# Twelve adaLN column steps moved from the projection blocks into the samples' unit of the recurrence

## The chip, the cores and the metric

The kernel runs on one core of one Trainium2 chip. The metric is the device time of one execution in microseconds (us). TensorE is called PE here (PEld is its weight load), VectorE DVE, ScalarE ACT, GpSimd POOL, and SyncE SP. SP issues nearly all DMA transfers of this kernel, one after the other in program order.

## The reference, cut to what matters

One layer of a streaming encoder: 2048 prompt positions and 8 samples of 16 positions. A small matrix product (adaLN) turns the 9 condition vectors (1 prompt, 8 samples) into six vectors of 1024: shift, scale and gate of the mixer (`sh1, sc1, g1`) and of the FFN (`sh2, sc2, g2`). The second half of them is needed late: `g1` at the output projection, `sh2` and `sc2` at the second norm, `g2` at the end.

```python
mod = jax.nn.silu(c) @ p['w_ada'][l] + p['b_ada'][l]
sh1, sc1, g1, sh2, sc2, g2 = jnp.split(mod[:, None], 6, axis=-1)
h = _rmsnorm(x, p['norm_mix'][l]) * (1.0 + sc1) + sh1
proj = h @ p['w_in'][l]
u_gate, u_lru, p_rwkv, u_s5 = jnp.split(proj, IN_SPLITS, axis=-1)
...
y_b, rw_shift, rw_s = _rwkv7(p_rwkv, rw_shift, rw_s, ...)      # the recurrence
...
mix = jnp.concatenate([y_a, y_b, y_c], axis=-1) @ p['w_out'][l]
x = x + g1 * mix
h2 = _rmsnorm(x, p['norm_ffn'][l]) * (1.0 + sc2) + sh2
f, ffn_buf = _conv_ffn(h2, ffn_buf, ...)
x = x + g2 * f
```

## The kernel before, in words

The work runs in four parts.

**Setup** computes `sh1` and `sc1` (tiles `sh1`, `gs1`), the vectors that the first norm needs.

**Projection blocks.** Four blocks of 512 positions (the first also holds the samples). Each block has 20 column groups of `w_in`: `gemm_cols` issues 24 matmuls into the tile `pgm` (a product in three parts, L558 to L560), then calls `bg_step`, which takes one or two closures from the list `bg` and runs them. That list holds work that needs no fixed place: tables for the S5 group, the sample states, the first chunks of the recurrence, and 32 adaLN steps (`ada_step`). One adaLN step makes 128 columns: it loads 512 KB of `w_ada` (tile `aw`, one buffer, L1218; the step asks for the next load when it is done), multiplies (8 matmul instructions into `pada`, L159, two records each in the profile), copies to `part` on ACT, multiplies again with a selector (`padm`, L164 or L172), and DVE adds the bias (L167 or L177). The projections of the RWKV group go on to `prep` (four calls a block, one after the other, `qr` and `bk` with one buffer each), whose last matmul writes `pb` (L693).

**Recurrence.** Nine units: unit 0 is the samples, then eight halves of the prompt's blocks. A unit has four chunks `c`. Ahead of a unit stands `inverse` (a triangular inverse in many small DVE instructions, L1190 to L1205, fed by a DMA round trip `tscr`, `tb`), and `join`, which turns its result into `xt`. In a unit PE does, per chunk: `st_q` (L1477 in unit 0), `st_u` (`um`, L1495), a part of the masks of a later unit (`pam`, L1155, operands `qr`, `bk` loaded by SP), `st_m` (`mm`), `st_y` (`ry`, L1529), and the next chunk's `pre_pe` (`pvt`, `pbk`) and `pre_v` (`ry`, L1457). Between these stands `fill`, three times a chunk, which steps the inverse of the next unit and pieces of the output projection.

In unit 0 PE's order is exactly the order of the code (`manual_schedule`). Everywhere else, and on the other engines in unit 0 too, a scheduler fixes each engine's order when the kernel is built. Each engine then works through its list in that order and waits at an instruction whose inputs or buffers aren't ready. `ppt` in the recurrence gives tiles from a pool of two PSUM buffers, in turn.

**FFN.** From about 1640 us on, with its own norm, up and down projections.

Of the kernel before, what the change touches and what calls it, by code (L numbers as in the profile page):

```python
# [9 lines left out]
F32 = mybir.dt.float32  # L10
# [9 lines left out]
P = 128  # L20
D = 1024
KD = D // P
# [14 lines left out]
def hymba_step(ctx: ExitStack, tc: tile.TileContext, I: dict, O: list):  # L37
    nc = tc.nc
    V, S, G, PE, SY = nc.vector, nc.scalar, nc.gpsimd, nc.tensor, nc.sync
# [3 lines left out]
    NBLK = SEQ // 512  # L43
# [4 lines left out]
    def act(out, in_, func=AF.Copy, **kw):  # L48
        S.activation(out, in_, func, **kw)  # L49
# [102 lines left out]
    s5fin = ct([P, 2, 8, 8], "s5fin")  # L152
    dcol = ct([P, 16], "dcol")

    def ada_cols(q, c_0, n, wt, psum, part, small):

        pg_ = psum("pada")
        for k in range(KD):
            PE.matmul(pg_[32 * (k % 4):32 * (k % 4) + 32, :n], lhsT=cT[:, k, :], rhs=wt[:, k, :],  # L159
                      start=(k < 4), stop=(k >= 4), skip_group_check=True)  # L160
        act(part[:, :n], pg_[:, :n])
        pm = psum("padm")
        if q in (2, 5):
            PE.matmul(pm[0:9, :n], lhsT=sel, rhs=part[:, :n], start=True, stop=True)  # L164
            bg_, gr_ = small("abg", n), small("agr", n)
            SY.dma_start(out=bg_, in_=I["b_ada"][:, q * D + c_0:q * D + c_0 + n].to_broadcast([9, n]))
            V.tensor_tensor(gr_, pm[0:9, :n], bg_, ADD)  # L167
            SY.dma_start(out=gmd[:, q // 3, c_0:c_0 + n], in_=gr_)
            return
        nm = n // P  # L170
        for m in range(nm):
            PE.matmul(pm[:, m * 9:m * 9 + 9], lhsT=part[:, m * P:(m + 1) * P], rhs=sel, start=True, stop=True)  # L172
        pv_ = pm[:, :nm * 9].rearrange("p (m j) -> p m j", j=9)
        c8 = c_0 // P
        b0 = offs["b_ada"] + q * 8 + c8
        dst = {0: sh1, 1: gs1, 3: sh2, 4: gs2}[q][:, c8:c8 + nm, :]
        V.tensor_tensor(dst, pv_, vec[:, b0:b0 + nm].unsqueeze(2).to_broadcast([P, nm, 9]), ADD)  # L177
        if q in (1, 4):
            n0 = offs["norm_mix" if q == 1 else "norm_ffn"] + c8
            V.scalar_tensor_tensor(dst, dst, 1.0, vec[:, n0:n0 + nm].unsqueeze(2).to_broadcast([P, nm, 9]), ADD, MUL)  # L180
# [269 lines left out]
    with ExitStack() as cm:  # L450
# [7 lines left out]
        def ppt(name):  # L458
            return pp.tile([P, 512], F32, tag="pp", name=name)
# [15 lines left out]
        bg = []  # L475
# [733 lines left out]
            sto["xs"] = xs_  # L1209


        adaq = [(q, c * P) for q in (2, 4, 3, 5) for c in range(KD)]
        adaw = []

        def ada_load(i):
            q, c_0 = adaq[i]
# [4 lines left out]
        def ada_step(i):  # L1221
            q, c_0 = adaq[i]
            if i == 0:
                ada_load(0)
            wt = adaw[i]
            part = lp.tile([P, P], F32, tag="apart", name="apart")
            ada_cols(q, c_0, P, wt, ppt, part, lambda t_, n: lp.tile([9, n], F32, tag=t_, name=t_))
            if i + 1 < len(adaq):
                ada_load(i + 1)

        w_load()
# [12 lines left out]
        bg += [late_work] + [lambda l=l: tab_phasor(l) for l in ((0, 1, 2, 3, 4), (5,), (6,), (7,))]  # L1244
        bg += [lambda k=k: tab_wk(k) for k in range(8)] + [tab_load]
        bg += [lambda k=k: tab_toep(k) for k in range(0, 8, 2)]
        bg += [lambda i=i: ada_step(i) for i in range(len(adaq))]
        for blk in range(NBLK):
            units = ["s", "p"] if blk == 0 else ["p"]
            s5_in(blk)  # L1250
            if blk == min(2, NBLK - 1):
                bg = s0_steps + bg + row_steps
            if blk % 2 == 1:
                bg = s5_half(blk // 2) + bg
            if blk + 1 < NBLK:
                load_x(blk + 1)
            lo12 = shift_mix(blk, 12)
            lo13 = shift_mix(blk, 13)
            xwa = {}
            for u in units:  # L1260
                T = NS if u == "s" else 512
                c0_ = 0 if u == "s" else NS + blk * 512
                lo_ = lo12[u]
                act(lo_[0:64, :T], lo_[0:64, :T], AF.Tanh)

                su = "s" if u == "s" else ""
                xw = xmp.tile([P, T], F32R, tag="xw" + su, name="xw", bufs=1)
                xa = xmp.tile([P, T], F32R, tag="xa" + su, name="xa", bufs=1)
                act(xw[0:64, :], lo_[0:64, :T])
                act(xa[64:128, :], lo_[64:128, :T])  # L1270
                V.tensor_tensor(xw[64:128, :], lo_[0:64, :T], xw[0:64, :].bitcast(F32), SUB)
                V.tensor_tensor(xa[0:64, :], lo_[64:128, :T], xa[64:128, :].bitcast(F32), SUB)
                xwa[u] = (xw, xa)
                sg = lo13[u]
                act(sg[:, :T], sg[:, :T], AF.Tanh, scale=0.5)
                V.tensor_scalar(sg[:, :T], sg[:, :T], 0.5, 0.5, MUL, ADD)
                SY.dma_start(out=sgd[:, c0_:c0_ + T], in_=sg[:, :T])
            if blk == NBLK - 1:
                lru(blk, 0)
                lru(blk, 1)  # L1280
            for hp in range(4):
                xr, xk, xv = shift_mix(blk, hp), shift_mix(blk, 4 + hp), shift_mix(blk, 8 + hp)
                for u in units:
                    ui = 0 if u == "s" else blk + 1
                    prep(hp, u, ui, xr[u], xk[u], xv[u], *xwa[u])
            for j in range(2):
                if blk + 1 < NBLK:
                    lru(blk, j)
                    if j == 0:
                        norm_full(blk + 1)  # L1290
            if blk + 1 < NBLK:
                norm_split(blk + 1)
            if blk + 1 == NBLK - 1:
                xin.close()
                cxq = ctx.enter_context(ExitStack())
                xqs.append(cxq.enter_context(tc.tile_pool(reuse_waits="tile", name="xq", bufs=3, side="right")))
                rap.append(cra.enter_context(tc.tile_pool(reuse_waits="tile", name="ra", bufs=1, side="right")))
                msks.append(rat([P, 2, P], "mask_s"))
                G.tensor_copy(msks[0], mask)
                for row in range(2):  # L1300
                    for e in range(2):
                        G.memset(msks[0][64 * row:64 * row + 32, e, :].rearrange("p (s t) -> p s t", t=32)[:, 1:4:2, :], 0.0)
                st0 = a_start()
                inv0 = inverse(0, st0)
                bg += [lambda c=c: a_chunk(0, st0, c) for c in range(4)] + [lambda: next(inv0, None)] * 10
            if blk == NBLK - 1:
                bg_step(len(bg))
# [3 lines left out]
    if True:  # L1311
        ow = crs.enter_context(tc.tile_pool(reuse_waits="tile", name="ow", bufs=1))
        po = crs.enter_context(tc.tile_pool(reuse_waits="tile", name="po", bufs=1, space=PSUM))
# [10 lines left out]
        def ot(shape, name, bufs=1):  # L1324
            return ow.tile(shape, F32, tag=name, name=name, bufs=bufs)
# [461 lines left out]
        wos = [(0, p_, load_wo, i) for i, p_ in enumerate((0, 1, 2, 3, 5, 7, 10, 11))]  # L1787
        wos += [(p_ // 12, p_ % 12, split_wo, i) for i, p_ in enumerate((4, 7, 10, 12, 13, 14, 15, 16))]
        gnq = []
        jn = None  # L1790
        FL, FC = 3, 6
        for n, un in enumerate(units):
            with (tc.manual_schedule(engines={mybir.EngineType.PE}) if n in (0,) else ExitStack()):
                nx = units[n + 1] if n + 1 < len(units) else None
                nx2 = units[n + 2] if n + 2 < len(units) else None
                for c in range(4):
# [4 lines left out]
                    def fill(pos):  # L1801

                        nonlocal inv, jn
                        for u_, p_, fn, k in wos:
                            if (u_, p_) == (n, pos):
                                fn(k)
                        if n == 3:
                            step(srg)
                        if inv is not None:
                            if not step(inv[1]):  # L1810
                                jn = join(inv[0], sto[inv[0]])
                                inv = None
                        if jn is not None and pos >= JP and not step(jn):
                            jn = None
                        if gnq and n > 0 and not step(gnq[0]):
                            gnq.pop(0)
                        o_step(OS)
                        if n == len(units) - 1:
                            if pos == FL:
                                nst.pop(0)()  # L1820
                            if pos >= FC:
                                for fn in nst[:5]:
                                    fn()
                                del nst[:5]
# [43 lines left out]
    with ExitStack() as cf:  # L1868
# [467 lines left out]
        with tc.manual_schedule(engines={ENG.PE, ENG.DVE, ENG.Activation, ENG.Pool, ENG.SP}):  # L2336
# [172 lines left out]
            turn, out = state_items(hal2.rearrange("p t m -> p (t m)"), 88, p_fc.rearrange("l b t (k p) -> (l b t k) p", p=P))  # L2509
# [9 lines left out]
            for k, (which, q, first, final) in enumerate(prods):  # L2519
# [56 lines left out]
                if xt is not None:  # L2576
                    t, n = done_of(k)
# [41 lines left out]
```

## Time and profile before

| | |
|---|---|
| median of 3 runs | 3210.2 us (3208.82 to 3218.33) |
| the profiled execution | 3212.56 us, its span 3210.8 us |
| PE busy | 2876.3 us, 90% of the span |
| DVE busy | 2115.3 us, 66% |
| ACT busy | 1373.9 us, 43% |
| POOL busy | 594.1 us, 19% |
| mean granted clock of PE | 0.917 |

The span runs from the first to the last instruction of the profiled execution. Busy times are sums over instructions; PE's are modelled, so a busy PE can still be a slow one. The granted clock is a share of 2.4 GHz: 1.00 is that level, 0.50 is 1.2 GHz.

### The profile page before, as it was taken

How to read it: one execution, taken by the hardware profiler on the slowest of the kernel's cores; microseconds unless marked ns; L12 is line 12 of the kernel's file. 1: busy time of each engine (PE TensorE's matmuls, PEld its weight loads, DVE VectorE, ACT ScalarE, POOL GpSimd, SP SyncE). 2: the span in 40 equal slices, each digit the busy share in tenths (PEclk: the TensorE clock that was granted, in tenths of full speed). 3: DMA queues.
4: the chain of work that ended last, by engine and by line, in shares of the span. 5: the costliest groups of instructions: out<-in, count | busy, mean ns of one | idle time of the engine just before them, and what ended most of it. 6: DMA issues, size and time to landing. Idle time of an engine off the chain costs nothing. (4 is left out here: it accounts for less than half of the span.)

```text
span 3210.8 us, 44566 instructions
## 1 busy us (share of the span) xinstructions
PE 2876.3 (90%) x16111; PEld 2292.9 (71%) x16111; DVE 2115.3 (66%) x3944; ACT 1373.9 (43%) x2436; POOL 594.1 (19%) x787
## 2 busy tenths in 40 slices
PE   5887996989977899999975999999599999899998
PEld 3766663756656778778754888888488887678876
DVE  6765774556666636766426777788888888364676
ACT  2445545553633324333444454444444444233222
POOL 1211201111234556666530000000000000000001
PEclk9988997989955779998977999999799999999999
DMA  6666554755574344443453333324333333576564
GB/s 182 140 104 151 162 150 139 216 145 172 160 197 135 82 127 135 133 123 100 121 174 112 114 107 117 101 79 120 107 107 99 104 103 118 185 241 224 175 218 172
DMA packets 595200, 453.45 MB, mean 141 GB/s; under 512 B 128032, under 2 KB 513700, under 8 KB 594980
## 3 DMA queue, kind: packets, MB, share of 16 engines
q1 hardware_dynamic: 594980, 450.60, 48.4%
q8 instruction: 127, 2.08, 0.3%
q14 instruction: 93, 0.76, 0.1%
HBM read 324.91 MB, written 125.59 MB: 140 GB/s over the span
## 5 line engine op out<-in xcount | busy, mean ns | idle before, releaser
L558 PE MATMUL pgm<-hhi,wh 128*128 128x512 f32 (+1 forms) x800 | 300.6, 376 | 3.1 <-ACT hhi L49 2.5
L560 PE MATMUL pgm<-hhi,wl 128*128 128x512 f32 (+1 forms) x800 | 297.0, 372 | 4.8 <-DVE wl L542 4.8
L559 PE MATMUL pgm<-hlo,wh 128*128 128x512 f32 (+1 forms) x800 | 299.9, 376 | 0.4 <-DVE hlo L521 0.4
L2140 PE MATMUL pu<-hht,ah 128*128 128x512 f32 x704 | 280.0, 398 | 1.1 <-DVE ub L2205 1.1
L2300 PE MATMUL pd<-dh,mh 128*128 128x512 f32 x660 | 261.2, 396 | 21.9 <-ACT mh L49 21.9
L2142 PE MATMUL pu<-hht,al 128*128 128x512 f32 x704 | 278.1, 395 | 0.0
L2141 PE MATMUL pu<-hlt,ah 128*128 128x512 f32 x704 | 277.7, 394 | 0.0
L2140 PE MATMUL pu<-hh,ah 128*128 128x512 f32 x528 | 212.9, 403 | 65.3 <-ACT ua L49 62.1
L2302 PE MATMUL pd<-dh,ml 128*128 128x512 f32 x660 | 261.4, 396 | 6.8 <-DVE ml L1888 6.8
L2301 PE MATMUL pd<-dl,mh 128*128 128x512 f32 x660 | 260.4, 395 | 0.8 <-DVE dl L1888 0.8
L1991 DVE SCALAR_TENSOR_TENSOR y<-us,fcw,y 128x1024 f32<-128x1024 f32 x176 | 225.0, 1279 | 0.8
L2240 POOL TENSOR_TENSOR sqa<-sqa 128x1 f32<-128x1 f32 x17 | 3.3, 193 | 1179.9 <-ACT full L49 1179.9
L2142 PE MATMUL pu<-hh,al 128*128 128x512 f32 x528 | 209.0, 396 | 0.0
L2141 PE MATMUL pu<-hl,ah 128*128 128x512 f32 x528 | 208.8, 395 | 0.0
L49 ACT ACTIVATE ah<-s 128x512 fp32r<-128x512 f32 x176 | 108.5, 629 | 213.1 <-DVE s L1932 187.8
L1199 DVE TENSOR_TENSOR xtmp<-xb,tb 128x2 f32<-128x2 f32 (+30 forms) x263 | 172.2, 655 | 39.8 <-POOL tb L1191 32.4
L1888 DVE TENSOR_TENSOR ml<-mr,mh 128x1408 fp32r<-128x1408 f32 x60 | 97.5, 1624 | 144.4 <-ACT mh L49 144.3
L1888 DVE TENSOR_TENSOR al<-s,ah 128x512 fp32r<-128x512 f32 x176 | 121.1, 689 | 92.6 <-ACT ah L49 67.6
L559 PEld LDWEIGHTS pgm<-hlo,wh 128*128 128x128 f32 x800 | 156.0, 195 | 35.1 <-issue 14.8
L558 PEld LDWEIGHTS pgm<-hhi,wh 128*128 128x128 f32 x800 | 156.3, 196 | 33.3 <-issue 10.2
L560 PEld LDWEIGHTS pgm<-hhi,wl 128*128 128x128 f32 x800 | 155.2, 194 | 32.7 <-issue 8.2
L2140 PEld LDWEIGHTS pu<-hh,ah 128*128 128x128 f32 x528 | 100.4, 190 | 88.8 <-ACT ua L49 62.7
(702 smaller groups left out, 6710.3 us busy)
## 6 DMA issues: line engine op xcount, KB each, us to landing
uwr<-in_ffn_up_dram SPq DMA_DIRECT2D x176, 256.0 KB
wr<-in_w_in_dram SPq DMA_DIRECT2D x80, 512.0 KB
mr<-mdd SPq DMA_DIRECT2D x56, 704.0 KB
dr<-in_ffn_down_dram SPq DMA_DIRECT2D x93, 256.0 KB
mdd<-ms SPq DMA_DIRECT2D x88, 256.0 KB
mdd<-y SPq DMA_DIRECT2D x66, 256.0 KB
xt<-in_x_prompt_dram SPq DMA_DIRECT2D x32, 512.0 KB
aw<-in_w_ada_dram SPq DMA_DIRECT2D x32, 512.0 KB
```

What stands on the lines that cost most here:

```text
L558: PE.matmul(o_, lhsT=whi[:, k, :], rhs=hh, start=(k == 0), stop=False)
L559: PE.matmul(o_, lhsT=whi[:, k, :], rhs=hl, start=False, stop=False)
L560: PE.matmul(o_, lhsT=wlo[:, k, :], rhs=hh, start=False, stop=(k == KD - 1))
L1199: V.tensor_tensor(tmp[:, :n, :t + 1], xb[:, :n, 0:t + 1], a, MUL)
L1888: eng.tensor_tensor(raw_lo, src, raw_hi.bitcast(F32), SUB)
L1991: V.scalar_tensor_tensor(y, us2[:, g, k:k + T], w_, y, MUL, ADD)
L2140: PE.matmul(pt, lhsT=a[0][:, k, :], rhs=b[0][:, k, :], start=start and k == 0, stop=False, skip_group_check=True)
L2141: PE.matmul(pt, lhsT=a[0][:, k, :], rhs=b[1][:, k, :], start=False, stop=False, skip_group_check=True)
L2142: PE.matmul(pt, lhsT=a[1][:, k, :], rhs=b[0][:, k, :], start=False, stop=(k == 3), skip_group_check=True)
L2300: PE.matmul(pt, lhsT=m[0][:, j, :], rhs=b[j][0], start=(j == 0), stop=False)
L2301: PE.matmul(pt, lhsT=m[0][:, j, :], rhs=b[j][1], start=False, stop=False)
L2302: PE.matmul(pt, lhsT=m[1][:, j, :], rhs=b[j][0], start=False, stop=(j == NH - 1))
```

## The change

The order of the four groups of adaLN columns becomes gate 1, gate 2, scale 2, shift 2. The first 16 steps stay in `bg`, as before. Steps 16 to 19 are put on `bg` after the last `prep` of the last block. Steps 20 to 31 run in unit 0: `fill` calls `ada_fill` at each of its twelve places there, which does the first half of one step and, at the next call, its second half (`ada_rows`). Their weights come into three buffers (tags `yh`, `yl`, `g1t`), three loads ahead; `pada` takes the buffer `po`, `padm` takes one of the two buffers of `ppt`.

```diff
-    def ada_cols(q, c_0, n, wt, psum, part, small):
+    def ada_cols(q, c_0, n, wt, psum, part, small, defer=None):
...
         act(part[:, :n], pg_[:, :n])
+        if defer:
+            defer(lambda: ada_rows(q, c_0, n, psum, part, small))
+        else:
+            ada_rows(q, c_0, n, psum, part, small)
+
+    def ada_rows(q, c_0, n, psum, part, small):
         pm = psum("padm")
...
-        adaq = [(q, c * P) for q in (2, 4, 3, 5) for c in range(KD)]
+        adaq = [(q, c * P) for q in (2, 5, 4, 3) for c in range(KD)]
         adaw = []
+        ADA_B, ADA_R = 16, 20
...
-            if i + 1 < len(adaq):
+            if i + 1 < ADA_R:
                 ada_load(i + 1)
...
-        bg += [lambda i=i: ada_step(i) for i in range(len(adaq))]
+        bg += [lambda i=i: ada_step(i) for i in range(ADA_B)]
...
+            if blk == NBLK - 1:
+                bg += [lambda i=i: ada_step(i) for i in range(ADA_B, ADA_R)]
...
+        adar, adap = [], []
+
+        def ada_ahead():
+            i = ADA_R + len(adar)
+            if i < len(adaq):
+                q, c_0 = adaq[i]
+                wt = ow.tile([P, KD, P], F32, tag=("yh", "yl", "g1t")[len(adar) % 3], name="awr")
+                SY.dma_start(out=wt, in_=I["w_ada"][0][:, q * D + c_0:q * D + c_0 + P].rearrange("(k p) c -> p k c", p=P))
+                adar.append((i, wt))
+
+        def ada_fill():
+            while adap:
+                adap.pop(0)()
+            if adan[0] < len(adar):
+                i, wt = adar[adan[0]]
+                adan[0] += 1
+                q, c_0 = adaq[i]
+                ada_cols(q, c_0, P, wt, lambda name: (po.tile([P, 512], F32, tag="po", name=name) if name == "pada"
+                                                      else ppt(name)),
+                         ot([P, P], "sgl", 2), None, adap.append)
+                ada_ahead()
+        adan = [0]
+        for _ in range(3):
+            ada_ahead()
...
+                        if n == 0 or adap:
+                            ada_fill()
```

The change moves instructions on every engine, since the scheduler builds the lists anew. Three places matter below.

SP at the end of the last block, before: `qrd`, `bkd`, `lamd` and `bod` are what a `prep` stores, `qb` are the loads for the masks of the first prompt unit, `xt` belongs to unit 0.

```order
L674 DMA bkd<-bk 1024x1x128
L684 DMA lamd<-nsb 2x16x32
L707 DMA vd<-xm 512x1x128
L699 DMA bod<-bon 128x4x128
L1208 DMA xscr<-xb 1024x1x32 x2
L1136 DMA qb<-bkd 128x512
L666 DMA qrd<-qr 1024x1x128
L1135 DMA qb<-qrd 128x512
L1136 DMA qb<-bkd 128x512
L1135 DMA qb<-qrd 128x512
L674 DMA bkd<-bk 1024x1x128
L684 DMA lamd<-nsb 2x16x32
```

The same place with the change:

```order
L672 DMA qrd<-qr 1024x1x128
L680 DMA bkd<-bk 1024x1x128
L690 DMA lamd<-nsb 2x16x32
L705 DMA bod<-bon 128x4x128
L1225 DMA aw<-in_w_ada_dram 128x8x128 x3
L1141 DMA qb<-qrd 128x512
L1142 DMA qb<-bkd 128x512
L1141 DMA qb<-qrd 128x512
```

All eight `qb` loads now stand behind the last `prep`'s stores and behind three `aw` loads, of which each waits until PE has done with the one buffer of the load before it.

PE in unit 0 from the first chunk's `um` to the second chunk's, before:

```order
L1495 MATMUL um<-rsb,xt__8568 64x64 x8
L1155 MATMUL pam<-qr,bk 128x128 x8
L1508 MATMUL mm<-bkt_8670,uv 64x64 x8
L1508 MATMUL mm<-bkt_8672,uv 64x64 x8
L1529 MATMUL ry<-uv,am 64x64 x8
L1437 MATMUL pbk<-ident,cqb 128x128 x4
L1457 MATMUL ry<-uv,am 128x64 x8
L1477 MATMUL ry<-sst,cqb 32x128 x16
L1495 MATMUL um<-rsb,xt__8568 64x64 x8
```

The same place with the change:

```order
L159 MATMUL pada<-awr,cT 32x128 x8
L1504 MATMUL um<-rsb,xt__8372 64x64 x8
L1161 MATMUL pam<-qr,bk 128x128 x8
L178 MATMUL padm<-sel,sgl 128x9
L159 MATMUL pada<-awr,cT 32x128 x8
...
L1446 MATMUL pbk<-ident,cqb 128x128 x4
L1466 MATMUL ry<-uv,am 128x64 x8
L178 MATMUL padm<-sel,sgl 128x9
L159 MATMUL pada<-awr,cT 32x128 x8
L1486 MATMUL ry<-sst,cqb 32x128 x16
L178 MATMUL padm<-sel,sgl 128x9
L159 MATMUL pada<-awr,cT 32x128 x8
```

A `pada` stands ahead of each `um` and behind other stages, with the `padm` of the step before. The second `padm` takes the PSUM buffer of the first one.

DVE at the end of the inverse of the first prompt unit, before (L1205 is its last instruction, L1551 starts the group norm of unit 0):

```order
L1199 TENSOR_TENSOR xtmp<-xb,tb 128x15x31
L1200 TENSOR_REDUCE xb<-xtmp 128x15
L1199 TENSOR_TENSOR xtmp<-xb,tb 128x512
L1200 TENSOR_REDUCE xb<-xtmp 128x16
L1205 TENSOR_TENSOR xb<-xb,lamc 128x512
L1551 TENSOR_REDUCE gs_9466<-ysb 128x8
```

The same place with the change (`gs_109` is the scale tile that the adaLN steps fill):

```order
L1205 TENSOR_TENSOR xtmp<-xb,tb 128x15x31
L1206 TENSOR_REDUCE xb<-xtmp 128x15
L1205 TENSOR_TENSOR xtmp<-xb,tb 128x512
L1206 TENSOR_REDUCE xb<-xtmp 128x16
L1211 TENSOR_TENSOR xb<-xb,lamc 128x512
L183 TENSOR_TENSOR gs_109<-padm,vec 128x9
L186 SCALAR_TENSOR_TENSOR gs_109<-gs_109,vec 128x9
```

DVE reads the first `padm` of unit 0 only after the whole inverse.

On SP, the first three `awr` loads of unit 0 stand behind the loads for all four of its chunks and the `tscr` stores that follow them, where the kernel before starts to load `wor`.

## Rows read from the trace of the kernel before

**Rows 1.** Stretches: PE, PEld, DVE, ACT, POOL busy us (instructions), PE clock, DMA share, GB/s.

```profile
760.00:896.00 136.00, 133.45 (x627) 92.20 (x626) 96.80 (x234) 71.22 (x117) 26.68 (x41) 1.00 0.51 146
896.00:920.00 24.00, 16.68 (x58) 10.36 (x57) 18.89 (x46) 7.60 (x14) 3.98 (x9) 0.56 0.71 207
920.00:970.00 50.00, 33.44 (x242) 29.17 (x241) 25.21 (x55) 10.71 (x17) 20.66 (x26) 0.50 0.95 229
970.00:1019.00 49.00, 45.42 (x462) 40.89 (x463) 20.76 (x26) 22.11 (x34) 25.96 (x21) 0.50 0.48 131
1019.00:1100.00 81.00, 66.24 (x549) 56.74 (x548) 54.49 (x121) 25.13 (x48) 39.89 (x41) 0.69 0.37 101
1100.00:1630.00 530.00, 493.88 (x4178) 407.97 (x4176) 302.69 (x548) 194.89 (x375) 313.04 (x308) 0.90 0.42 122
```

**Rows 2.** Waits of PE and PEld, 640 to 780: us, times, longest.

```profile
PE pada L159 <- DMA aw<-in_w_ada_dram: 6.7, 5, 3.5
...
PEld pada L159 <- DMA aw<-in_w_ada_dram: 1.9, 1, 1.9
```

**Rows 3.** Timeline of all engines around two adaLN steps: start, us, instruction, idle before.

```profile
665.95 0.39 PE L559 MATMUL pgm<-hlo,wh 128*128 128x512 f32 x1
...
666.27 0.64 PE L159 MATMUL pada<-aw,cT 128*32 128x128 f32 x16
...
667.16 0.52 SPq L1218 DMA_DIRECT2D aw<-in_w_ada_dram  x1
...
668.11 0.40 PE L558 MATMUL pgm<-hhi,wh 128*128 128x512 f32 x1
668.34 0.40 PE L559 MATMUL pgm<-hlo,wh 128*128 128x512 f32 x1
...
672.43 0.65 PE L159 MATMUL pada<-aw,cT 128*32 128x128 f32 x16 [0.27 <-DMA aw<-in_w_ada_dram]
```

**Rows 4.** Timeline of PE: an adaLN step at the lower clock.

```profile
707.08 1.08 PE L159 MATMUL pada<-aw,cT 128*32 128x128 f32 x16
```

**Rows 5.** PE: last projection matmuls (880 to 930), first and last `pb` of the block.

```profile
L560 PE MATMUL pgm<-hhi,wl x18: 387/389/500, 880.0 to 896.4; 128*128 128x512 f32 x18
...
875.27 0.50 PE L693 MATMUL pb<-rkl,bones 128*128 128x512 f32 x1
...
918.87 0.79 PE L693 MATMUL pb<-rkl,bones 128*128 128x512 f32 x1
```

**Rows 6.** Timeline of SP's DMA issues, last block to unit 0.

```profile
920.84 2.17 SPq L1354 DMA_DIRECT2D xt__8568<-xscr  x4
...
927.78 7.90 SPq L1165 DMA_DIRECT2D tscr<-am  x8
...
956.64 1.03 SPq L1165 DMA_DIRECT2D tscr<-am  x2
...
964.62 0.43 SPq L1136 DMA_DIRECT2D bk<-bkd  x1
```

**Rows 7.** Timeline of DVE: start and end of the inverse of the first prompt unit.

```profile
945.48 2.10 DVE L1190 TENSOR_TENSOR tb<-tb,lam 128x1024 f32<-128x1024 f32 x1 [20.66 <-DMA tb<-tscr]
...
981.62 0.69 DVE L1205 TENSOR_TENSOR xb<-xb,lamc 128x512 f32<-128x512 f32 x1
```

**Rows 8.** Timeline of PE in unit 0.

```profile
937.79 1.97 PE L1495 MATMUL um<-rsb,xt__8568 64*64 64x64 f32 x16 [0.71 <-ACT rsb L49]
...
954.89 1.93 PE L1477 MATMUL ry<-sst,cqb 128*32 128x128 f32 x32
...
970.75 2.04 PE L1155 MATMUL pam<-qr,bk 64*128 64x128 f32 x8 [11.19 <-DMA bk<-bkd]
...
1016.71 1.97 PE L1529 MATMUL ry<-uv,am 64*64 64x64 f32 x16
```

**Rows 9.** Timeline of PE and of DVE in the first prompt unit.

```profile
1039.07 1.97 PE L1495 MATMUL um<-rsb,xt__9110 64*64 64x64 f32 x16 [6.52 <-ACT rsb L49]
...
1017.34 0.96 DVE L1199 TENSOR_TENSOR xtmp<-xb,tb 128x2 f32<-128x2 f32 x1 [11.29 <-POOL tb L1191]
```

## The prediction

> **What bounds the kernel now.** I read the table of busy time by stretch first, since the change takes work from one stage and puts it in another. From 760 to 896 us, in the last projection block, PE is busy 133.45 of 136 us at the full clock [rows 1]: each PE instruction less there is time gained, as far as the end of the block is set by PE. From 896 to 920 us only the last `prep` runs: DVE is busy 18.89 of 24 us, PE 16.68, and PE's clock falls to the lower level (1.2 GHz). Unit 0 of the recurrence lies from about 928 to 1019 us, all at 0.50: first with the DMA engines 0.95 busy, then with PE busy 45.42 of 49 us [rows 1]. So PE isn't idle in unit 0; its work is slow. From 1100 to 1630 us PE is busy 493.88 of 530 us [rows 1], so a late end of unit 0 isn't made up by slack later.
>
> Next I read the timelines of the engines in unit 0, to see who waits for whom. DVE sits idle 20.66 us until the inverse's input `tb` has landed, starts the inverse at 945.48 and ends it at 981.62 + 0.69 = 982.31 [rows 7]. PE meanwhile works through unit 0's first chunk, and waits once for long: 11.19 us for `bk`, which SP issued at 964.62 [rows 6, 8]. The last stage of unit 0 ends at 1016.71 + 1.97 = 1018.68 [rows 8].
>
> I call the end of the last `prep` (its last `pb`) t: 918.87 + 0.79 = 919.66 [rows 5]. In these terms, before: SP goes on to unit 0's loads at t + 1.2 and to the `tscr` stores at t + 8.1; the inverse ends at t + 62.7; unit 0 ends at t + 99.0.
>
> **Part 1: sixteen steps leave the blocks.** Around one step, six `pgm` matmuls start from 665.95 to 668.11, five intervals in 2.16 us; without a step an interval is 0.23 us, so the step costs 2.16 - 1.14 = 1.0 us of PE [rows 3]. Sixteen cost 16 us. PE and PEld also wait 6.7 + 1.9 us for the weights from 640 to 780 us [rows 2]; about five of the steps stay in that stretch and keep some of it, so I take 6 of the 8.6. The last projection matmul, which ended at 896.4 + 0.4 = 896.8 [rows 5], comes 22 us sooner (bounds 14 and 27). Not all of that reaches t. The four `prep` of the last block end 14.5 us apart ((918.87 - 875.27) / 3) [rows 5], since each is a chain through PE, ACT and DVE with one set of buffers; before, one stands behind the last matmul, and with the change PE's list has two there. So t moves from 896.8 + 22.9 to 874.8 + 1 + 2 x 14.5 = 904.8: **15 us gained** (bounds 8 and 22).
>
> **Part 2: four steps at the end of the last block.** Step 16 has its weights early. Each later one is a round: the load lands 5.3 us after its issue (667.16 to 672.43 [rows 3]), the multiplication at the lower clock takes 1.08 [rows 4], then SP may issue the next. SP issues the first at about t + 1.3 (behind `bod`) and the third at t + 1.3 + 2 x 6.4 = t + 14.1. Behind it stand the eight `qb` loads, some 4 us of issues, so unit 0's loads begin at t + 18.6 and not at t + 1.2: 17.4 us later. The `qb` data (2 MB, at the 207 to 229 GB/s of [rows 1] some 9 us) lands at about the time when they are needed; I add 1.6 for that. **19 us lost** (bounds 16 and 23). Queued behind these waits: on SP all loads of unit 0 and `tscr`, so the inverse; on PE all masks from `qb`.
>
> **Part 3: twelve steps in unit 0.** Two locks hold PE there. The first is the weights. Their place on SP's list is where `wor` was, 956.64 + 1.03 - 927.78 = 29.9 us behind the start of `tscr` [rows 6]; with part 2 that is t + 8.1 + 19 + 29.9 = t + 57, and they land at about t + 63. PE's first `pada` stands ahead of the first `um`, which otherwise could run at about t + 37. From that `pada` to the second `padm` PE needs 954.89 - 937.79 = 17.1 [rows 8] and 2.5 for two `pada` and a `padm`: t + 82.6. The second lock is DVE: the second `padm` takes the PSUM buffer that DVE frees only after the whole inverse, at t + 62.7 + 19 = t + 81.7. Both open at the same time, so removing one of them would not help much. The place of the second `padm` is that of 954.89 in the kernel before, t + 35.2; now it is t + 82.6.
>
> From there the rest of unit 0 took 1018.68 - 954.89 = 63.8 us. Of this the 11.19 us for `bk` are gone, as SP is past its old backlog. Ten `pada` at 1.08 [rows 4] and eleven `padm`, by estimate 0.4 each (a single 128x512 `pgm` takes that [rows 3]), come in: 15.2. Three waits like the 0.71 for `rsb` [rows 8] are covered by them: -2.1. New waits come from SP's list: the `qr` and `bk` of the second chunk stand behind an `awr` load that waits for the fourth `pada`; 1.5 us of issues and the 6.1 us that `bk` took (964.62 to 970.75 [rows 6, 8]), less a `um` of 2.0, are 5.6, and about 4 more for the last chunk. I take 10 (bounds 0 and 16). Sum: 63.8 - 11.2 + 15.2 - 2.1 + 10 = 75.7. With t = 904.8 unit 0 ends at 904.8 + 82.6 + 75.7 = 1063.1: **44 us later** than 1018.7.
>
> **Part 4: what comes back.** In the first prompt unit PE waits 6.52 us for `rsb`, behind group norm work on ACT and DVE that stands among an inverse which POOL held up 11.29 us [rows 9]. With unit 0 longer, POOL's splits of `wor` are done and that inverse begins well ahead of the unit's end. I give back these 6.5 (bounds 0 and 12). ACT's copies and DVE's adds of the twelve steps lie beside PE's work and cost nothing of their own while PE is the last; the order of the adaLN groups costs nothing, since `gs2` and `sh2` are first read in the last unit.
>
> **Sum.** 44 - 6.5 = 37.5 us on the profiled execution's 3212.6 gives 3250.1. That execution lies 2.4 us above the median of the runs, so the forecast is 3248 us. With the bounds, the forecast's own range is 3218 to 3280.
>
> **Rivals.** (a) *PE's clock rises in unit 0* (chance 0.17, faster). The place is 928 to 1100 us, where the clock is 0.50 and then 0.69. If the added matmuls brought the full clock, the 65 us of PE work behind the second `padm` would take 33, and the first prompt unit's 66 us [rows 1] some 18 less: 37.5 - 32 - 18 = -12.5, so 3198. It decides from a clock of about 0.9 in unit 0. Against it: from 970 to 1019 us PE is busy 93% and stays at 0.50 [rows 1]; the new `pada` are fewer than the matmuls there. The Trainium skill, TensorE: Matmul & The Clock Gate, section "HAM oscillation", has the rule for it: idle gaps throttle the array, and a kernel that keeps the array fed keeps its clock. By that rule filling waits would pay; this stretch of the trace does not bear it out.
>
> (b) *The losses and gains cancel* (0.13, within 0.3%). Part 1 at its bound (7 more), part 2 at its bound (3 less), no new waits on `bk` (10 less), and the first prompt unit free of all its 15 us of waits (81 - 66.24 [rows 1], 8.5 more than I gave) leave 37.5 - 28.5 = 9, so 3219. For it: the parts share one cause, how early DMA loads arrive, so they lean the same way.
>
> (c) *Every `awr` load is late* (0.08, slower still). Nine later loads come three ahead; if each held PE for half a landing, 2.7 us, that is 24 more, 3272 or above. Against it: three chunks' worth of stages, some 20 us at the lower clock, lie between an issue and its use.
>
> The forecast has 0.62. A difference of 0.3%, 9.6 us, is about what a measurement of this kernel tells from no change. Slower by more holds the forecast and (c), 0.70; the same 0.13; faster 0.17. The range of 8 in 10 goes from 3206, which leaves out (a) and a little, to 3280.
>
> **What the profile after would show.** Part 1: the last `pgm` near 875 us, and the last `pb` near 905. Part 2: three `aw` issues some 6.4 us apart behind the last `bod`, and PE's `pada` there waiting for each. Part 3: PE idle for 20 us or more ahead of the first `pada<-awr`, or of the second `padm` until DVE's inverse has ended; unit 0's last `ry` (L1529 before) near 1063, and a wait for `bk` in the second chunk of 5 to 8 us. Part 4: the wait for `rsb` in the first prompt unit gone. The forecast is wrong if the `awr` loads land before the first `um` is ready and DVE reads `padm` in time, if the clock in unit 0 is above 0.5, or if the end of unit 0 moves and the recurrence's end near 1640 us does not.

## The result, and the profile after

| | before | changed |
|---|---|---|
| median | 3209.5 us | 3253.3 us (4 runs, 3236.4 to 3258.3) |
| the profiled execution | 3212.6 us | 3252.3 us, span 3250.4 us |
| mean granted clock of PE | 0.917 | 0.903 |

The ratio is 1.0121, with a 95% interval of 1.008 to 1.0162: the change costs some 39 us (26 to 52). The forecast was 3248 us. Two executions of over 5100 us, one of the kernel before and one of experiment 7, are left out of the ratios and ranges below. Lines of the changed kernel are 6 to 9 higher than before: `padm` is read by DVE in L183, `aw` is loaded in L1225 and `awr` in L1807, unit 0's `ry` is L1538, the mask matmuls (`pam`) are L1161, the inverse is L1196 to L1211.

The first view is the table of stretches, with the columns of [rows 1].

```profile
760.00:896.00 136.00, 112.43 (x467) 73.75 (x463) 89.46 (x186) 69.44 (x110) 14.55 (x35) 0.88 0.45 127
896.00:920.00 24.00, 16.82 (x108) 15.29 (x108) 6.90 (x19) 0.88 (x3) 2.27 (x4) 0.50 0.86 223
920.00:970.00 50.00, 28.95 (x236) 25.08 (x240) 31.71 (x69) 8.97 (x17) 19.48 (x25) 0.50 0.84 206
970.00:1019.00 49.00, 41.77 (x414) 35.72 (x406) 6.40 (x16) 19.46 (x33) 14.98 (x14) 0.55 0.62 165
1019.00:1050.80 31.80, 13.86 (x227) 12.31 (x227) 20.39 (x48) 6.26 (x11) 19.95 (x14) 0.53 0.37 122
1050.00:1110.00 60.00, 60.00 (x352) 53.67 (x351) 24.65 (x41) 17.93 (x34) 25.34 (x26) 0.50 0.24 60
```

PE's 133.45 busy us from 760 to 896 have become 112.43: the blocks end earlier. But from 920 to 970, where PE was busy 33.44 us before, it is busy 28.95, although matmuls were added there; and from 1019 to 1050.8 it is busy 13.86 of 31.8. So unit 0 now has more waiting in it than before, not less.

The timeline of SP shows why it starts late (rows as in [rows 6]).

```profile
894.59 5.51 SPq L1225 DMA_DIRECT2D aw<-in_w_ada_dram  x2
900.15 0.57 SPq L1141 DMA_DIRECT2D qb<-qrd  x1
...
905.27 2.97 SPq L1363 DMA_DIRECT2D xt__8372<-xscr  x4
...
914.65 6.50 SPq L1171 DMA_DIRECT2D tscr<-am  x8
...
944.78 3.24 SPq L1807 DMA_DIRECT2D awr<-in_w_ada_dram  x3
```

The loads of unit 0 begin (`xt`, 905.27) 17.5 us behind the last `pb` (887.76, below), and not 1.2 us behind it; the first `awr` are issued 57 us behind it. The timeline of PE from the last `pb` to the end of unit 0 and the first `um` of the next unit shows what that does:

```profile
886.96 0.80 PE L699 MATMUL pb<-rkl,bones 128*128 128x512 f32 x1
...
893.46 1.08 PE L159 MATMUL pada<-aw,cT 128*32 128x128 f32 x16 [4.14 <-DMA aw<-in_w_ada_dram]
...
950.03 1.08 PE L159 MATMUL pada<-awr,cT 128*32 128x128 f32 x16 [19.27 <-DMA awr<-in_w_ada_dram]
...
967.68 0.59 PE L178 MATMUL padm<-sel,sgl 128*128 128x9 f32 x2
...
979.60 2.04 PE L1161 MATMUL pam<-qr,bk 64*128 64x128 f32 x8 [5.16 <-DMA bk<-bkd]
...
1024.75 2.04 PE L1161 MATMUL pam<-qr,bk 64*128 64x128 f32 x8 [3.41 <-DMA bk<-bkd]
...
1045.11 1.91 PE L1392 MATMUL px<-xt__9049,wt 32*32 32x32 f32 x62 [13.67 <-DVE sh L183]
...
1048.86 1.97 PE L1538 MATMUL ry<-uv,am 64*64 64x64 f32 x16
...
1062.54 1.96 PE L1504 MATMUL um<-rsb,xt__9049 64*64 64x64 f32 x16
```

PE waits 19.27 us for `awr`; the waits for `bk` are 5.16 and 3.41 and not one of 11.19 [rows 8]; and a wait of 13.67 us stands ahead of `px`, a part of the join near the end of unit 0. Its releaser is the read of a `padm` in L183. The timeline of DVE (rows as in [rows 7]) has the reason:

```profile
931.33 1.23 DVE L1196 TENSOR_TENSOR tb<-tb,lam 128x1024 f32<-128x1024 f32 x1 [12.80 <-DMA tb<-tscr]
...
963.79 0.93 DVE L1211 TENSOR_TENSOR xb<-xb,lamc 128x512 f32<-128x512 f32 x1
964.64 0.15 DVE L183 TENSOR_TENSOR gs<-padm,vec 128x9 f32<-128x9 f32 x1
...
1030.78 0.96 DVE L1205 TENSOR_TENSOR xtmp<-xb,tb 128x2 f32<-128x2 f32 x1 [8.45 <-POOL tb L1197]
...
1044.89 0.16 DVE L183 TENSOR_TENSOR sh<-padm,vec 128x9 f32<-128x9 f32 x1
```

The first `padm` of unit 0 is read at 964.64, right behind the whole inverse. A later one, multiplied at 1029.59, is read only at 1044.89: DVE had begun the next inverse, which itself waited 8.45 us for POOL, and the read stands in the middle of it. `px` needs the PSUM buffer that this read frees.

### The profile page after: what moved, and what is told of

Read it like the earlier page. It is cut to its first block, busy times and chain, and to the rows that moved or that the text cites. A ratio compares the mean times of both kernels' runs of the same rounds, so it can differ in the third digit from the quotient of the medians.

```text
span 3250.4 us, 44582 instructions
## 1 busy us (share of the span) xinstructions
PE 2894.0 (89%) x16111; PEld 2312.3 (71%) x16111; DVE 2116.8 (65%) x3944; ACT 1373.0 (42%) x2436; POOL 590.1 (18%) x787
## 5 line engine op out<-in xcount | busy, mean ns | idle before, releaser
L1205 DVE TENSOR_TENSOR xtmp<-xb,tb 128x2 f32<-128x2 f32 (+30 forms) x263 | 168.3, 640 | 35.3 <-POOL tb L1197 27.9
L2336 PEld LDWEIGHTS pd<-dh,mh 128*128 128x128 f32 x660 | 126.6, 192 | 51.0 <-ACT mh L49 24.8
```

The costliest lines, as they stand in the source:

```text
L1205: V.tensor_tensor(tmp[:, :n, :t + 1], xb[:, :n, 0:t + 1], a, MUL)
L2336: PE.matmul(pt, lhsT=m[0][:, j, :], rhs=b[j][0], start=(j == 0), stop=False)
```

## The experiments

Twelve kernels were run in three groups (1 to 4, 5 to 8, 9 to 12; the middle group on another chip than the other two), each beside the kernel before, whose median was 3204.2, 3203.9 and 3204.5 us. Differences in us are (ratio - 1) times 3204; a ratio's interval reaches some 0.2 to 0.4% to either side. Single executions of the kernel before ranged there from 3185 to 3222 us, and each trace is of one execution, up to 25 us from its kernel's median (experiment 5), so the traces are compared by lengths inside them. The table takes them from each trace's timeline of PE: the end of the last `pb`, the time from there to the end of unit 0 (the last of its `ry` in `st_y`), and the time from there to the end of the last unit. The last `pb` is not the same point of the work in all of them: the masks of the first prompt unit (`pam<-qb`, 64 matmul instructions, some 12 us of PE at the lower clock) stand partly ahead of it in the kernel before, 4 and 12, wholly ahead of it in 1, 3, 8 and 11, and wholly behind it in the changed kernel and in 2, 5, 6, 7, 9 and 10. What moves across it is the same work counted in another column.

| kernel | median us | ratio (interval) | last `pb` | to unit 0's end | units 1 to 8 |
|---|---|---|---|---|---|
| before | 3209.5 | 1 | 919.7 | 99.0 | 608.8 |
| changed | 3253.3 | 1.0121 (1.008, 1.0162) | 887.8 | 163.1 | 617.2 |
| 1 no late steps | 3184.6 | 0.9955 (0.9926, 0.9983) | 901.0 | 98.7 | 600.6 |
| 2 end of block alone | 3208.7 | 1.0012 (0.9988, 1.0037) | 895.4 | 118.6 | 608.8 |
| 3 unit 0 alone | 3239.9 | 1.0116 (1.008, 1.0152) | 901.7 | 136.8 | 609.3 |
| 4 order alone | 3206.3 | 0.9998 (0.9972, 1.0024) | 909.5 | 99.3 | 602.7 |
| 5 early weights | 3248.8 | 1.0112 (1.0072, 1.0153) | 885.9 | 162.9 | 593.9 |
| 6 ACT adds the bias | 3221.4 | 1.0036 (1.0014, 1.0059) | 893.4 | 143.3 | 609.7 |
| 7 both (5 and 6) | 3213.0 | 1.0027 (1.0007, 1.0046) | 889.9 | 142.7 | 598.1 |
| 8 both, 20 in blocks | 3205.4 | 1.0002 (0.9983, 1.002) | 906.9 | 118.1 | 596.9 |
| 9 DVE free, early | 3214.3 | 1.0026 (1.0003, 1.0048) | 893.3 | 133.6 | 604.0 |
| 10 DVE free, behind `tscr` | 3209.4 | 1.0009 (0.9985, 1.0034) | 896.6 | 137.0 | 612.9 |
| 11 the same, 20 in blocks | 3200.8 | 0.9988 (0.9967, 1.0009) | 908.0 | 110.6 | 597.2 |
| 12 the same, 26 in blocks | 3206.0 | 1.0012 (0.9987, 1.0036) | 913.3 | 102.9 | 618.4 |

**1. Steps 16 to 31 left out.**

```diff
-        ADA_B, ADA_R = 16, 20
+        ADA_B, ADA_R = 16, 16
+        adaq = adaq[:16]
...
+        G.memset(gs2, 0.0)
+        G.memset(sh2, 0.0)
```

> Steps 16 to 31 are left out (gs2 and sh2 are set to 0, so the FFN's input is not the reference's). Theory (the loss is a sum of places: the blocks end 32 us sooner, all else is loss behind them): the last pb ends near 888, unit 0 takes 99 us from there as in the kernel before and ends near 987, the whole near 3180 us (3172 to 3190). Rival (PE's clock decides: the steps' absence does not bring the clock back): unit 0 ends near 987 too, but the first prompt unit stays at 0.50 and takes 67 us and not 60, the whole 3187 or more. Rival (sixteen steps are worth only the 15 us of the forecast): 3195.

Measured: 14 us less than before by the ratio (5 to 24), 20 by the medians. That is near the forecast's 15 and not 32. Unit 0 takes 98.7 us from the last `pb`, as in the kernel before, so no loss of the change is left behind it. The early `pb` of the changed kernel's profile, 887.8, is 5 us better than the mean: the eight kernels with 16 steps in the blocks have it at 885.9 to 901.0, mean 892.9, the two with 32 at 909.5 and 919.7, mean 914.6. The 901.0 is this experiment's, where PE does all the masks of `qb` ahead of it, here in PE's timeline:

```profile
876.73 3.10 PE L1161 MATMUL pam<-qb 64*128 64x128 f32 x16
...
883.80 6.64 PE L1161 MATMUL pam<-qb 64*128 64x128 f32 x32
...
892.18 3.09 PE L1161 MATMUL pam<-qb 64*128 64x128 f32 x16
...
900.39 0.63 PE L699 MATMUL pb<-rkl,bones 128*128 128x512 f32 x1
```

In the changed kernel they stand behind it:

```profile
906.17 11.64 PE L1161 MATMUL pam<-qb 64*128 64x128 f32 x64 [0.27 <-DMA qb<-bkd]
```

Kernels 1 and 2 leave out work and so compute something else, but behind the recurrence their traces take as long as the others (1582.3 and 1585.6 us; 1583.3 before).

**2. Only steps 16 to 19 at the end of the block.**

```diff
         ADA_B, ADA_R = 16, 20
+        adaq = adaq[:20]
...
+        G.memset(gs2, 0.0)
+        G.memset(sh2, 0.0)
```

> Steps 16 to 19 stand at the end of the last block as in the change; steps 20 to 31 are left out (sh2 and half of gs2 are 0, so the FFN's input is not the reference's). Theory (the serial weight loads delay qb, tscr and the inverse): 18 us more than without all sixteen, unit 0 ends near 1005, the whole near 3198 us (3190 to 3206). Rival (the rounds lie beside loads of unit 0 that PE would wait for anyway): 5 us more or less, near 3185.

Measured: 3208.7, and 118.6 us from the last `pb`. Against experiment 1 the four steps cost 18 us by the ratios (some 12 to either side, so the rival's 5 us is out, though narrowly). By the traces it is 118.6 - 98.7 = 19.9 from the last `pb`, which holds the masks that moved across it; unit 0's end itself moved from 999.7 to 1013.9, 14 us. The four steps at the end of the block give back all that the blocks gain.

**3. Only steps 20 to 31 in unit 0.**

```diff
-        ADA_B, ADA_R = 16, 20
+        ADA_B, ADA_R = 20, 20
```

> Steps 16 to 19 go back into the blocks (20 steps there, nothing at the end of the last block), 20 to 31 stay in unit 0. Theory (PE in unit 0 is locked by the weights' late place on SP's list and by DVE's inverse ahead of the first padm read): the last pb ends near 897 (four steps at 2.3 us), the inverse ends 63 us behind it, unit 0 ends 83 us behind that, near 1043, the whole near 3242 us (3230 to 3252). Rival (the rounds at the end of the block are the loss, and filling unit 0 costs little once they are gone): unit 0 ends near 1015, the whole near 3212.

Measured: 3239.9; the last `pb` at 901.7, unit 0's end at 1038.5. Without the serial loads ahead of it, unit 0 still takes 136.8 us and not 99. Experiment 1 has the masks in the same place, so the twelve steps cost 136.8 - 98.7 = 38.1 us in unit 0. The rival (3212) is out: most of the loss is in unit 0.

**4. The order of the groups alone.**

```diff
-        ADA_B, ADA_R = 16, 20
+        ADA_B, ADA_R = 32, 32
```

> Only the order of the four groups of columns is changed; all 32 steps stay in the blocks. Theory: nothing reads these vectors before the output projection, so the same as before, 3210 us within 8. Rival (the change of order moves the writes of gmd and the loads of the bias rows into a busier place): 3220 or more.

Measured: 0.9998, with an interval of 8 us to either side. No cost of the order shows.

**5. The weights of unit 0 early.** The block of code with `ada_ahead` and its three first calls moves up.

```diff
+        for _ in range(3):
+            ada_ahead()
         units = [0] + list(range(2, 2 * NU))
         qbs = []
...
-        for _ in range(3):
-            ada_ahead()
```

> The first three loads of awr are issued ahead of the qb loads, before all loads of unit 0. Counted from the last pb, unit 0 ends 99 us later in the kernel before and 163 us later with the change. Theory of the prediction (two locks on PE that open at the same time, the weights and DVE's inverse, so that taking one away does little): PE no longer waits for awr, but for the PSUM buffer of the second padm until the inverse has ended; 3 us gained, unit 0 ends near 160 us behind the last pb, the whole near 3245 us where the change itself would stand at 3249 (3238 to 3252). Rival (the weights alone hold PE): 19 us gained, near 3230 or less.

Measured: 1.0112, no less than the change within the intervals, and unit 0 is as long (162.9). Both are what the theory forecast, but not by its mechanism: PE does not wait at the second `padm`. The timeline of DVE in this run says why:

```profile
939.42 0.17 DVE L183 TENSOR_TENSOR gs<-padm,vec 128x9 f32<-128x9 f32 x1 [18.10 <-PE padm L178]
...
951.13 0.17 DVE L183 TENSOR_TENSOR gs<-padm,vec 128x9 f32<-128x9 f32 x1 [11.15 <-PE padm L178]
...
952.34 1.21 DVE L1196 TENSOR_TENSOR tb<-tb,lam 128x1024 f32<-128x1024 f32 x1
...
985.26 0.16 DVE L183 TENSOR_TENSOR gs<-padm,vec 128x9 f32<-128x9 f32 x1
```

With early weights the scheduler put DVE's reads of the first two `padm` ahead of the inverse. They waited 18.10 and 11.15 us for PE, and the inverse began at 952.34 and not at 931.33. The two engines now wait for each other. In PE's timeline the second `padm` comes 64.6 us behind the last `pb` and not 79.9, so early weights gain 15.3 us there; behind it most of that is lost again, by a wait for `bk` of 9.37 us (5.16 in the change) and by 8.46 us ahead of a `pbk` until the read at 985.26 frees a buffer. The wait ahead of `px` is still there, 14.80:

```profile
950.50 0.59 PE L178 MATMUL padm<-sel,sgl 128*128 128x9 f32 x2
...
965.79 2.04 PE L1161 MATMUL pam<-qr,bk 64*128 64x128 f32 x8 [9.37 <-DMA bk<-bkd]
...
985.57 1.09 PE L1470 MATMUL pbk<-ident,cqb 128*128 128x128 f32 x4 [8.46 <-DVE gs L183]
...
1043.06 1.91 PE L1416 MATMUL px<-xt__9049,wt 32*32 32x32 f32 x62 [14.80 <-DVE sh L183]
```

**6. ACT reads `padm` in unit 0.**

```diff
-        V.tensor_tensor(dst, pv_, vec[:, b0:b0 + nm].unsqueeze(2).to_broadcast([P, nm, 9]), ADD)
+        if small is None and nm == 1:
+            act(dst[:, 0, :], pm[:, 0:9], AF.Identity, bias=vec[:, b0:b0 + 1])
+        else:
+            V.tensor_tensor(dst, pv_, vec[:, b0:b0 + nm].unsqueeze(2).to_broadcast([P, nm, 9]), ADD)
```

> In unit 0 ACT and not DVE reads padm and adds the bias, so no PSUM buffer waits for a DVE that is within an inverse; the weights stay late. Theory of the prediction (two locks on PE): at the second padm nothing is gained, since the weights hold PE as long; but the wait of 13.7 us for DVE ahead of px at the end of unit 0, which the prediction did not have, goes: unit 0 ends near 150 us behind the last pb, the whole near 3236 us (3228 to 3244). Rival (px waits for something else as well, its own operands): 3 us gained or less, 3246 or more.

Measured: 3221.4, a gain of some 27 us on the change (ratios 1.0121 and 1.0036, so some 15 to either side), more than the 13 expected; the rival's 3 is out. From PE's timeline:

```profile
954.37 1.08 PE L159 MATMUL pada<-awr,cT 128*32 128x128 f32 x16 [18.57 <-DMA awr<-in_w_ada_dram]
...
972.02 0.59 PE L178 MATMUL padm<-sel,sgl 128*128 128x9 f32 x2
...
1030.98 1.92 PE L1395 MATMUL px<-xt__9049,wt 32*32 32x32 f32 x64
...
1056.72 1.96 PE L1507 MATMUL um<-rsb,xt__9049 64*64 64x64 f32 x16 [9.30 <-ACT rsb L49]
```

The weights hold PE as before (18.57), and the second `padm` comes 78.6 us behind the last `pb`, where it came 79.9 in the change. So at that place DVE's read wasn't what PE waited for. The wait ahead of `px` is gone, and unit 0 is 163.1 - 143.3 = 19.8 us shorter: 13.7 of that is `px`; of the rest a part is a stretch at a higher clock (0.88 from 990 to 1000 us), and I didn't separate it. A wait for `rsb` of 9.30 us is back in the next unit.

**7. Both edits.** The diffs of 5 and 6 together.

> Early loads of awr and ACT for the bias, together. Theory of the prediction: both locks open, so the second padm comes about 19 us sooner than in the change, and px does not wait for DVE: unit 0 ends near 130 us behind the last pb, the whole near 3216 us (3208 to 3226), more than the two edits give apart. Rival (PE's clock or the loads of bk, qr and xt are what sets unit 0's pace): the sum of the two edits apart or less, 3230 or more.

Measured: 3213.0, 36 us less than early weights alone and 8 us less than the ACT edit alone by the medians; by the ratios 27 and 3. So early weights add nothing to the ACT edit that the intervals tell from zero. The whole lies in the theory's range (3208 to 3226), but its mechanism did not occur: unit 0 took 142.7 us and not 130, about as with the ACT edit alone (143.3). In the trace the scaling of `gs2`, still on DVE, again stands ahead of the inverse, which began at 957.14, and PE waits 10.83 us for `bk`.

**8. Both, and steps 16 to 19 back in the blocks.** The diffs of 5, 6 and 3 together.

> As both together, and steps 16 to 19 back in the blocks, so that no weights are loaded one by one at the end of the last block. Theory (a sum of places): another 18 us less behind the last pb and 6 us more ahead of it: unit 0 ends near 112 us behind the last pb, the whole near 3204 us (3196 to 3212), the same as before. Rival (the three early loads of awr, 1.5 MB, now take the place of the serial ones in front of unit 0's loads): 3215 or more.

Measured: 3205.4, no difference from before. Unit 0 is 142.7 - 118.1 = 24.6 us shorter than in 7, and the last `pb` 17.0 us later; some 12 us of both is the masks, which PE does here ahead of the last `pb`. Unit 0's end itself is 7.6 us earlier. The time is the theory's, 3204, and by the interval the rival's 3215 is out.

**9. DVE takes no part in unit 0's steps, weights early.** The diffs of 5 and 6, and in the new branch of 6:

```diff
+            if q == 4:
+                n1 = offs["norm_ffn"] + c8
+                act(dst[:, 0, :], dst[:, 0, :], AF.Identity, scale=vec[:, n1:n1 + 1], bias=vec[:, n1:n1 + 1])
+            return
```

> As early loads and ACT for the bias together, but ACT also does the scaling of gs2, so DVE takes no part in the steps of unit 0. Theory (in the two runs with early loads DVE's list had the reads of the first padm ahead of the inverse, which began 66 us behind the last pb and not 44): the inverse begins near 48 us behind the last pb, the wait of 10 us for rsb in the first prompt unit goes, and the whole is some 10 us less than the two together, near 3203 us (3196 to 3208). Rival (PE is held by the late loads of bk, whatever DVE does): as those two together, 3213.

Measured: 3214.3; the time is the rival's. The inverse does begin early, 49 us behind the last `pb` (893.28), and unit 0 is 9 us shorter than in 7. The whole is no shorter: the last `pb` came 3 us later and units 1 to 8 took 6 us more (604.0 and 598.1), which is within their spread, and the wait for `rsb` in the first prompt unit, which was to go, stays. The rows of DVE's and of PE's timeline:

```profile
942.26 1.23 DVE L1203 TENSOR_TENSOR tb<-tb,lam 128x1024 f32<-128x1024 f32 x1 [12.86 <-DMA tb<-tscr]
```

```profile
975.21 2.04 PE L1168 MATMUL pam<-qr,bk 64*128 64x128 f32 x8 [9.29 <-DMA bk<-bkd]
...
1047.69 1.97 PE L1535 MATMUL um<-rsb,xt__9049 64*64 64x64 f32 x16 [9.89 <-ACT rsb L49]
```

**10. The same, with the three early loads behind `tscr`.** The block with `ada_ahead` and its three calls moves up less far than in 5, to this place:

```diff
+        for _ in range(3):
+            ada_ahead()
         for c in range(1, 4):
             pls.append(pre_load(0, c))
```

> DVE free as above, and the three early loads of awr are issued behind tscr and not ahead of qb. Theory (1.5 MB ahead of qb cost 5 us of waiting for qb): the inverse begins 44 us behind the last pb, the first pada waits little; the whole near 3199 us (3191 to 3206). Rival (their bytes cost the same wherever they go): 3203 or more.

Measured: 3209.4, which is the rival's by the median; the interval reaches down to about the theory's 3199, so it is inconclusive. The wait for `qb` (5.74 us in 9) is gone and the inverse begins 42 us behind the last `pb`, but PE then waits 10.58 us for `bk`, and unit 0 (137.0) is no shorter.

**11. The same, and 20 steps in the blocks.** The diffs of 10 and 3 together.

> As before this, and steps 16 to 19 back in the blocks, so no serial weight loads at the end of the last block. Theory (a sum of places: 18 us less behind the last pb, 6 us more ahead of it): near 3190 us (3181 to 3198), faster than before by 14. Rival (with the locks gone unit 0 is full of PE work at 1.2 GHz, so twelve steps cost what they save): 3203 or more, no change from before.

Measured: 3200.8, ratio 0.9988 with an interval from 0.9967 to 1.0009: the lowest of those that compute everything, but not distinguished from before, as the rival had it. The forecast of 3190 lies outside the interval.

**12. The same, with 26 steps in the blocks.** `ADA_B, ADA_R = 26, 26`.

> As before this, with 26 steps in the blocks and only six in unit 0. Theory (a sum of places: six steps gain 1.3 us each ahead of the last pb and cost 1.5 us each in unit 0, less what they fill of its 20 us of waits): near 3196 us (3188 to 3204). Rival (all that counts is the waits that are filled, and six steps fill them as twelve do): 3190 or less.

Measured: 3206.0, no difference from before and above what both expected. Unit 0 is the shortest of those with steps in it (102.9), but the last `pb` is back at 913.3: ten more steps in the blocks than in 10 take 16.7 us there and give back 34.1 in unit 0, four of them as serial loads.

## Why the prediction was right, step by step

**The sum.** It put 15 us gained ahead of the last `pb` against 19 lost at the end of the block and some 40 lost in unit 0. The runs give, in that order: 14 gained (experiment 1 by its ratio; 22 by the mean of the last `pb` in the traces), 18 lost (2 against 1), and 35 lost (the change against 2, 39 less 4; 163.1 - 118.6 = 44.5 in the traces). The last is 38.1 by the traces of 3 against 1. Each of these ratios carries 9 to 15 us to either side. Within that the signs and sizes are right, by kernels that have one part alone, so the likeliest case was right and in the main for its reasons. In the profiled execution the terms missed by 5 to 17 us each, and four corrections follow.

**Part 1, the last projection matmul.** It was to come 22 us sooner; it came 28 sooner (mean end 864.2 in the eight kernels with 16 steps, 892.5 in the two with 32). The price of a step was low: from the groups of instructions up to the last `pgm`, 16 steps take 24.8 - 12.5 = 12.3 us of `pada` and 5.6 of `padm`, and 16.8 - 8.1 = 8.7 us of waits for `aw`, and not 16 and 6. First the kernel before, then the changed one:

```profile
L159 PE MATMUL pada<-aw,cT 128*32 128x128 f32 x512 | 24.8, 305 | 16.8 <-DMA aw<-in_w_ada_dram 16.8
L172 PE MATMUL padm<-sel,apart 128*128 128x9 f32 x64 | 13.0, 295 | 4.9 <-ACT apart L49 3.2 <-DVE ph L325 1.7
```

```profile
L159 PE MATMUL pada<-aw,cT 128*32 128x128 f32 x256 | 12.5, 314 | 8.1 <-DMA aw<-in_w_ada_dram 8.1
L178 PE MATMUL padm<-sel,apart 128*128 128x9 f32 x32 | 7.7, 350 | 4.7 <-ACT apart L49 3.2 <-DVE ph L331 1.5
```

(The `padm` of the other groups add 7.3 and 7.0.) That more `prep` stand behind the last matmul and keep part of this was right: from there to the last `pb` it is 27.9 us in the changed kernel, 22.9 before. In all the last `pb` came 22 us sooner by the means and 32 in the profiled pair, where the sum had 15: by the traces this term was sized too small (by experiment 1's ratio it is 14). Not all of it is gain, since 8.2 us of the masks (three groups of `pam<-qb` at 904.01, 912.40 and 916.90) stood ahead of the last `pb` in the kernel before and stand behind it now.

**Part 2** was right in sum: the loads of unit 0 began 17.5 us behind the last `pb` (forecast 18.6), 16.3 later than before; the inverse began 43.6 us behind it (931.33) where before it was 25.8 [rows 5, 7], that is 17.8 later. A round of load and multiplication was shorter than its 6.4 us: the three `aw` issues stand at 888.97, 894.59 and 899.73, 5.6 and 5.1 us apart.

**Part 3, the two locks.** The places were right: the first `pada` was to open at about 63 us behind the last `pb` and ran at 62.3, the second `padm` at 82.6 and ran at 79.9. But only the first lock held PE there. DVE's read ended 3 us ahead of that `padm`, which shows no wait. "Removing one of them would not help much" came out for the weights in the total (experiment 5), but by another way, the scheduler's new order of DVE's list. For DVE it was wrong (experiment 6): a DVE that reads `padm` between pieces of an inverse holds PE wherever PE next takes a buffer of that pool. The place that the prediction did not have is `px`, 13.67 us, in a sum that had 10 for new waits on `bk`, which came to 8.6. That is 12 us more than the sum had; unit 0 took 163.1 us from the last `pb` and not 158.3, 4.8 more: the second `padm` came 2.7 us sooner than forecast, and PE had a spell above the lower clock (0.55 from 970 to 1019), whose worth I didn't separate.

**Part 4, what comes back,** is the step that failed. The wait of 6.52 us for `rsb` [rows 9] is gone (the `um` at 1062.54 shows none), yet the first prompt unit took 67.2 us, from 1050.83 to 1118.0, and not 60.4 - 6.5 = 53.9. The sum took the rest of this unit over as it was and put a change of the clock there at nothing; the mean granted clock over the unit was 0.75 before (1018.7 to 1079.1) and 0.53 now. PE is busy 60.00 of 60 us there at the lower clock, where before it rose to the full one from 1055 on:

```profile
1040.00:1055.00 15.00, 15.00 (x92) 13.63 (x91) 12.66 (x16) 4.51 (x9) 10.18 (x7) 0.50 0.08 18
1055.00:1080.00 25.00, 23.82 (x251) 20.61 (x249) 11.13 (x23) 11.83 (x24) 16.42 (x20) 0.98 0.47 112
```

(the table of stretches of the kernel before). How much of that is the change's is not settled: units 1 to 8 took 594 to 618 us over the 14 traces with no order by what was changed. In the profiled execution the misses cancel: the last `pb` came 17.0 us sooner than forecast (887.8 for 904.8), unit 0 took 4.8 us more, and units 1 to 8 took 617.2 and not 608.8 - 6.5 = 602.3, 14.9 more. That its total, 3252.3, came within 2.2 us of the 3250.1 is therefore luck; that it came out slower by tens of us is not.

**The rivals.** (a) did not occur: unit 0 was at 0.50 for most of its length, 0.55 from 970 to 1019. The rule cited from the Trainium skill, TensorE: Matmul & The Clock Gate, section "HAM oscillation", speaks of idle gaps that throttle the array. It does not tell what happened in the first prompt unit, where PE was 60.00 of 60 us busy from 1050 to 1110, without a gap in the profile, and stayed at 0.50. (b) and (c) were not reached; in the changed kernel no `pada` behind the first waits for its `awr`.

**Why no version wins.** With DVE out of the steps, earlier weights and no serial loads (experiment 11) unit 0 is still 110.6 us long, 11.9 more than in experiment 1, which has the masks in the same place and no steps in unit 0. PE does the twelve steps there at a mean clock of 0.57 (928 to 1020 us), waits again for `bk` (10.04 us), as before the change [rows 8], and still twice for `awr` (3.28 and 5.40). That the blocks gain per step about what unit 0 loses per step is argued from this; within what these runs can tell, the whole is the same.

## What to carry to other kernels

Work that is moved into a stage "where an engine waits" lands in that stage's queues: ask for each new instruction what it stands behind on its DMA queue and which slow neighbour must free its buffer, and look for every later place that takes a buffer of the same pool. Take one of two locks away and the other, or the scheduler's new order, may take its place; test them apart and together. And price the part by kernels that have it alone, counted from a point that the change does not move: the last `pb` here had some 12 us of masks ahead of it in one kernel and behind it in the next, and the totals agreed better than the terms.

## What the runs showed of the hardware that was not expected

The spread of one program: the kernel before ran 29 times beside the first group, from 3185.4 to 3221.6 us, a range of 1.1% and not the 0.3% that its first three runs suggested; its mean granted clock was 0.923 in the shortest and 0.915 in the longest. And PE's clock did not rise alike behind work that looks alike: in the changed kernel PE was 60.00 of 60 us busy at 0.50 (1050 to 1110, 352 matmuls), where in the kernel before 15.00 of 15 us at 0.50 (1040 to 1055, 92 matmuls) were followed by 0.98 (1055 to 1080). Why is open; no run here was made to tell.
